# Interleaved chunks that ask for the third quarter last but one, an embedding group in other banks, and the final norm's rows loaded a stage later

## The chip, the core and the metric

The kernel runs on one core of a Trainium2 chip. The metric is device time in microseconds (us) of one execution; lower is better. TensorE (PE) multiplies into PSUM banks; its weight loads are shown apart as PEld. VectorE (DVE) and ScalarE (ACT) do the elementwise work and empty the banks. GpSimd (POOL) and SyncE (SP) here mostly issue DMA transfers.

## The reference, cut to what matters

Two layers over 256 tokens of width 2048, all in fp32. A layer mixes tokens, projects back, adds to the residual, and then adds a per-layer embedding that is gated by a third product of the same width:

```
hn = rmsnorm(h, norm)
u  = hn @ w_in                      # layer 0: 2048 x 6144, layer 1: 2048 x 8208
y  = token mixing of u              # HGRN2 and RG-LRU in layer 0, mLSTM in layer 1
h  = h + y @ w_out                  # 2048 x 2048
pl = rmsnorm(p[i] @ ple_w[i], ple_norm[i])          # 256 -> 2048, the "embedding"
h  = h + sigmoid(h @ ple_gate_w[i]) * pl            # 2048 x 2048, the "gate"
...
return rmsnorm(h, final_norm)
```

## The kernel before, in words

**Products.** A weight arrives as a 128 x 1024 tile `raw` (SP issues the load), is split by ACT into a rounded high part `whi` (L135) and by DVE into the rest `wlo` (L136), and each output is the sum of three products, high by high, high by low and low by high (L196 to L198 in `quarter_tok`, L217 in the seven-product stages). There are four `whi`, four `wlo` and five `raw` buffers. A *chunk* is 512 output columns for the 256 tokens, in two banks (one per 128 tokens); it is built in four *quarters* of the 2048 inputs, 24 matmuls and two weight tiles each.

**Banks.** Of the PSUM banks three form the ring `mm` (pool `pm`), three the ring `mx` (pool `px`), two are `st`. A ring hands out its banks in turn, and a matmul that opens a bank waits until the bank's former contents have been read.

**Stages.** Layer 1 ends with: the gate projections `oog` and `oz` (`seven`, which for each pair of chunks opens banks A, E and B of the `mm` ring and F of the `mx` ring, and whose last results are read out of E and B by L292), the embedding's product (`embed`, L472), the projection back (`out_proj` over the weights `oo`), and the last gate (weights `g1`). `embed` makes four column groups, each with one bank per half of the tokens: eight bank fillings of six matmuls. The first half's bank is copied out by ACT (L483), the second's by DVE (L481).

**Interleaved chunks.** A stage whose inputs come from the stage before cannot have them all at its start: the token-major results are transposed by DVE (L519, L649), sent to DRAM and back by POOL's transfers (`across`, L636 and L639), and turned by ACT and DVE into the split `act` pairs (L667, L149, L150 for `feature_major`; L535, L537 for `to_features`). So `project_two` works on the first two chunks at once, one in `mm` banks and one in `mx` banks, and `before(kq)` (made by `ready`) forces the pairs of quarter kq into the program before the first quarter that reads them. Five stages use it, by way of `chunks`: `eo` and `g0` of layer 0, `oqk`, `oo` and `g1` of layer 1.

**Order.** Small generators called lanes do this side work. `pump` advances each lane one step, once in each quarter, and a lane that has sent its transfers lets `lag` steps go by before it converts what comes back. The framework's scheduler then gives each engine one fixed order of instructions, from the order of the program and from priorities (the weight splits stand 400 places ahead, the embedding's copies 450). An engine works strictly down its list: an instruction that waits holds up all behind it. The lane `fm2` is the third of layer 1's four transposed results (the inputs of quarter 2 of `oo`), `fm3` the fourth. The lane `emb` squares the embedding (L402), multiplies it by its gain rows (L1413, the rows loaded by L503 on POOL's queue) and, before the change, ends by loading the final norm's two rows `fnr` with the same L503.

Of the kernel before, what the change touches and what calls it, by code (L numbers as in the profile page):

```python
# [43 lines left out]
def trunk(ctx: ExitStack, tc: tile.TileContext, a, out):  # L44
# [19 lines left out]
    def start(lane, gen):  # L64
        lanes.setdefault(lane, []).append(gen)
# [16 lines left out]
    def drain(*which):  # L82
        for lane in which:
            while step(lane):
                pass
# [84 lines left out]
    def project_two(w, act, before):  # L170

        ps = [[pool.tile([P, 512], F32, name=name, tag=name) for _ in range(2)]
              for pool, name in ((pm, "mm"), (px, "mx"))]
        for j, kq in ((0, 0), (0, 1), (0, 2), (1, 0), (1, 1), (1, 2), (0, 3), (1, 3)):
            before(kq)
            quarter_tok(w, j, kq, act, ps[j])
            if kq == 3:
                yield ps[j]

    def chunks(w, n, act, before):  # L180
        yield from project_two(w, act, before)
        for j in range(2, n):
            yield project_tok(w, j, act)
# [261 lines left out]
    def embed(w, pact, tile_of, first=None):  # L445

        pls = []
        for b in range(2):
            head = first and b == 0
            if head:  # L450
                part, pact = load_head(w[0])
                parts = [part] + load_weights(w[0], (1, 2), (1,))
            else:
                parts = load_weights(w[b], *(((2, 1),) if first else ()))
            if first and b:
                first()
            for c, (hi, lo) in enumerate(parts):
                terms = [(hf, k, x, y, 0, 512) for hf in range(2) for k in range(2) for x, y in ((0, 0), (0, 1), (1, 0))]
                if head:
                    terms.sort(key=(lambda t: (t[3], t[3] and t[0], t[1])) if c == 0 else  # L460
                               (lambda t: (t[1], t[3] if t[1] == 0 else t[0], t[3])))
                    if c == 0:
                        terms[0:4] = [(hf, 0, x, 0, o, T) for o in (0, T) for x in range(2) for hf in range(2)]
                pool, name = (px, "mx") if first and c == 0 else (pm, "mm")
                ps = [pool.tile([P, 512], F32, name=name, tag=name) for _ in range(2)]
                halves = []
                for n, (hf, k, x, y, o, w_) in enumerate(terms):
                    mine = [m for m, t in enumerate(terms) if t[0] == hf]
                    with ExitStack() as behind:
                        if first and "pe" in last:  # L470
                            behind.enter_context(tc.issue_after(last["pe"]))
                        last["pe"] = te.matmul(ps[hf][:, o:o + w_], tokens(pact[x], k, hf),  # L472
                                               (hi, lo)[y][:, k * 512 + o:k * 512 + o + w_],
                                               start=(n == mine[0]), stop=(n == mine[-1])).ins
                    if n < mine[-1]:
                        continue
                    pl = tile_of()
                    with ExitStack() as order:
                        order.enter_context(tc.high_priority(offset=600 if first else 450))
                        if hf and (b or not first):  # L480
                            ins = v.tensor_copy(pl, ps[hf]).ins  # L481
                        else:
                            ins = s.copy(pl, ps[hf]).ins  # L483
                        if not first:
                            last["out", hf] = ins
                    halves.append(pl)
                pls.append(halves)
        return pls
# [9 lines left out]
    def row(pool, tag, bufs, i):  # L498

        halves = []  # L500
        for b in range(2):
            t = pool.tile([P, 1024], F32, name="row", tag=tag, bufs=bufs)
            gp.dma_start(out=t, in_=a["rows"][i, b * 1024:(b + 1) * 1024].partition_broadcast(P))  # L503
            halves.append(t)
        return halves
# [8 lines left out]
    def to_features(h, c, act, gain, name, more=None):  # L514

        w = room("w")
        w5 = w.rearrange("p (j c h t) -> p h c j t", j=4, c=4, h=2)
        for hf in range(2):
            v.transpose(w5[:, hf], h[:, hf].rearrange("p (c j q) -> p c j q", c=4, j=4))  # L519
        r = room("r")  # L520
        yield from across(w, r, f"d{name}{c}", 6)
        r5 = r.rearrange("p (i c h t) -> p c h i t", i=4, c=4, h=2)
        for b in range(2):
            if gain:
                x = tp.tile([P, 512], F32, name="xr", tag="hn", bufs=3)
                for k in range(2):
                    s.activation(x[:, k * T:(k + 1) * T].rearrange("p (h i t) -> p h i t", h=2, i=4), r5[:, 2 * b + k],
                                 AF.Copy, scale=pc(gain, 4 * c + 2 * b + k))
                act[2 * c + b] = split_act(x, "h")
            else:  # L530
                hi, lo, both = act_pair()
                for k in range(2):
                    src = r5[:, 2 * b + k]
                    hk, lk = (x[:, k].rearrange("p (h i t) -> p h i t", h=2, i=4) for x in (hi, lo))
                    s.copy(hk, src)  # L535
                    for hf in range(2):
                        v.tensor_tensor(out=lk[:, hf], in0=src[:, hf], in1=hk[:, hf].bitcast(F32), op=ALU.subtract)  # L537
                act[2 * c + b] = (hi, lo, both)
        if more is not None:
            yield  # L540
            more(c, r5)

    def ready(act, lane):

        def before(kq):
            while 2 * kq + 1 not in act:
                step(f"{lane}{kq}")
        return before
# [111 lines left out]
    def feature_major(u, gain, first, y, lag):  # L660

        r = yield from landed((u[:, 0], u[:, 1]), f"du{gain}{first}", lag)
        r5 = r.rearrange("p (i c h t) -> p c h i t", i=4, c=4, h=2)
        for b in range(2):
            x = tp.tile([P, 512], F32, name="xr", tag="hn", bufs=3)
            for k in range(2):
                s.activation(x[:, k * T:(k + 1) * T].rearrange("p (h i t) -> p h i t", h=2, i=4), r5[:, 2 * b + k],  # L667
                             AF.Copy, scale=pc(gain, first + 2 * b + k))
            y[first // 2 + b] = split_act(x, "y")
# [55 lines left out]
    if True:  # L725
# [285 lines left out]
        y = {}  # L1011
# [117 lines left out]
    with tc.tile_pool(name="m1", bufs=2) as m1:  # L1129
# [229 lines left out]
        for jj in (0, 2):  # L1359
            us = [m1.tile([P, 2, 512], F32, name="u", tag="vt", bufs=6) for _ in range(2)]  # L1360
            for b, hf, src in pair(a["oz"], jj, not jj):
                j, u = jj + b, us[b]
                with tc.high_priority(offset=100):
                    s.activation(u[:, hf], src, AF.Tanh, scale=norm["rth"][:, hf:hf + 1])
                    v.scalar_tensor_tensor(u[:, hf], u[:, hf], 1.0, src, op0=ALU.add, op1=ALU.mult)
                for i in range(2):
                    c = hf * 8 + 2 * j + i
                    e = slice(i * 256, (i + 1) * 256)
                    v.scalar_tensor_tensor(u[:, hf, e], u[:, hf, e], fac[:, c:c + 1], nums[j][:, hf, e],
                                           op0=ALU.mult, op1=ALU.mult)  # L1370
                if hf:
                    start(f"fm{j}", feature_major(u, "cn", 4 * j, y, 5 + jj // 2))
        hq = []

        def home():
# [23 lines left out]
        def embed_norm():  # L1399
            yield  # L1400
            yield from ple_gain_squares()
            v.tensor_scalar(rp, rsqrt_cols(total(pss, 4)), 0.5, None, op0=ALU.mult)
            fnr.extend(row(m1, "vt", 6, 2))

        def ple_gain_squares():
            rows = row(m1, "vt", 6, 1)
# [18 lines left out]
        def gated(n, ps, tr, pl, hf, on_act=True):  # L1425
# [8 lines left out]
            else:  # L1434
# [2 lines left out]
                sq = tp.tile([P, 512], F32, name="sq", tag="sq", bufs=1)[:, 0:pl.shape[1]]  # L1437
                v.scalar_tensor_tensor(sq, pl, 1.0, pl, op0=ALU.mult, op1=ALU.mult, accum_out=o)

        warm = tp.tile([P, 1], F32, name="warm", tag="warm", bufs=1)  # L1440
        for g, ps in enumerate(chunks(a["g1"], 3, act, ready(act, "fo"))):
            for hf in range(2):
                pl = pls[g][hf]
                gated(g, ps[hf], hq[g][:, hf], pl, hf)
                v.tensor_tensor(out=pl, in0=pl, in1=fnr[g // 2][:, (g % 2) * 512:(g % 2 + 1) * 512], op=ALU.mult)
# [190 lines left out]
```

## Time and profile before

| | |
|---|---|
| time, median of 3 runs | 1029.7 us (1029.24 to 1032.07) |
| the profiled execution: time | 1030.27 us |
| its span, first to last instruction | 1028.5 us |
| PE busy | 1016.8 us (99%) |
| DVE, ACT, POOL busy | 796.4, 623.7, 101.7 us |
| granted TensorE clock, mean | 0.998 |
| DMA | 241.09 MB, mean 234 GB/s |

The profiled execution's time is its span and 1.77 us around it. In a timeline each row gives start, duration, engine, source line, operation, tiles, shape and count; the bracket says how long the engine sat idle before it and what ended that. Consecutive matmuls overlap in their records, so the pace of PE is read from start to start.

### The profile page before, as it was taken

What the parts mean: (1) busy time and instruction counts of PE and PEld (TensorE: products, weight loads), DVE (VectorE), ACT (ScalarE), POOL (GpSimd) and SP (SyncE); (2) the same over time, 40 slices, a digit from 0 to 9 for tenths busy, and PEclk for the clock granted to TensorE, in tenths of its full rate; (3) what the DMA queues carried; (4) which work ended last, traced back from release to release, by engine and by line L of the source; (5) the groups of instructions that cost most, each with busy time, mean ns of one, the idle gap of its engine ahead of it and who ended that gap; (6) DMA issues with size and microseconds to landing.
All of it is one profiled execution on the core that took longest, in us unless ns stands there. A gap on an engine that the chain in (4) does not pass through costs nothing.

```text
span 1028.5 us, 14493 instructions
## 1 busy us (share of the span) xinstructions
PE 1016.8 (99%) x5194; PEld 843.4 (82%) x5194; DVE 796.4 (77%) x1212; ACT 623.7 (61%) x893; POOL 101.7 (10%) x186
## 2 busy tenths in 40 slices
PE   9999999999999999999999999999999999999996
PEld 7888888888888888888888888887888878888886
DVE  7858968969685785767559987888999976766684
ACT  7675555686964345565457776666666666344562
POOL 0111101011112121021021100001011112111000
PEclk9999999999999999999999999999999999999999
DMA  9987756567688897798798756376975779798652
GB/s 360 336 243 231 220 172 204 174 197 236 227 264 291 275 286 230 237 302 256 228 284 244 237 173 203 127 246 173 286 182 170 235 248 348 230 304 255 197 185 82
DMA packets 69384, 241.09 MB, mean 234 GB/s; under 512 B 8992, under 2 KB 10400, under 8 KB 69312
## 3 DMA queue, kind: packets, MB, share of 16 engines
q1 hardware_dynamic: 55008, 194.41, 57.8%
q0 software_dynamic: 13872, 45.23, 15.4%
q8 instruction: 40, 0.66, 0.3%
q10 hardware_dynamic: 432, 0.52, 0.1%
q14 instruction: 32, 0.26, 0.1%
HBM read 220.21 MB, written 19.92 MB: 233 GB/s over the span
## 4 chain that ended last, share of the span: by engine, by line
PE 95%; DMA 2%; issue 1%; ACT 1%; DVE 0%; POOL 0%; ACTq 0%; DVEq 0%; POOLq 0%
PE mm L196 21%; PE mm L197 21%; PE mm L198 21%; PE mm L217 10%; PE mx L198 4%; PE mx L196 4%; PE mx L197 4%; PE mx L217 3%; PE nu L1277 1%; PE mm L1461 1%; PE mm L1462 1%; PE mm L1460 1%; DMA r<-ducn 1%; PE mm L472 1%; DMA ducn<-w 1%
## 5 line engine op out<-in xcount | busy, mean ns | idle before, releaser
L136 DVE TENSOR_TENSOR wlo<-raw,whi 128x1024 fp32r<-128x1024 f32 (+1 forms) x333 | 401.6, 1214 | 156.1 <-ACT whi L135 147.3
L135 ACT CAST whi<-raw 128x1024 fp32r<-128x1024 f32 (+1 forms) x333 | 347.8, 1048 | 262.5 <-PE mm L198 189.6
L196 PE MATMUL mm<-whi,ahl 128*128 128x512 f32 x960 | 375.2, 391 | 0.0
L197 PE MATMUL mm<-wlo,ahl 128*128 128x512 f32 x960 | 374.0, 390 | 0.0
L198 PE MATMUL mm<-whi,ahl 128*128 128x512 f32 x960 | 373.6, 389 | 0.0
L196 PEld LDWEIGHTS mm<-whi,ahl 128*128 128x128 f32 x960 | 180.2, 188 | 38.2 <-issue 0.8
L198 PEld LDWEIGHTS mm<-whi,ahl 128*128 128x128 f32 x960 | 180.2, 188 | 37.6
L197 PEld LDWEIGHTS mm<-wlo,ahl 128*128 128x128 f32 x960 | 180.3, 188 | 37.3 <-DVE wlo L136 0.6
L217 PE MATMUL mm<-whi,ahl 128*128 128x512 f32 x288 | 91.1, 389 | 0.0
L217 PEld LDWEIGHTS mm<-whi,ahl 128*128 128x128 f32 x288 | 54.1, 188 | 11.1
L196 PE MATMUL mx<-whi,ahl 128*128 128x512 f32 x160 | 62.2, 389 | 0.0
L197 PE MATMUL mx<-wlo,ahl 128*128 128x512 f32 x160 | 62.2, 389 | 0.0
L198 PE MATMUL mx<-whi,ahl 128*128 128x512 f32 x160 | 62.2, 389 | 0.0
L217 PE MATMUL mm<-wlo,ahl 128*128 128x512 f32 x144 | 56.2, 390 | 0.4 <-DVE wlo L136 0.4
L207 DVE TENSOR_TENSOR wlo<-ch,whi 128x1024 fp32r<-128x1024 f32 x34 | 41.0, 1220 | 6.0 <-ACT whi L206 5.4
L206 ACT CAST whi<-ch 128x1024 fp32r<-128x1024 f32 x34 | 35.6, 1052 | 6.4 <-PE mm L217 3.7
L198 PEld LDWEIGHTS mx<-whi,ahl 128*128 128x128 f32 x160 | 30.0, 188 | 6.2
L197 PEld LDWEIGHTS mx<-wlo,ahl 128*128 128x128 f32 x160 | 30.0, 188 | 6.2
L196 PEld LDWEIGHTS mx<-whi,ahl 128*128 128x128 f32 x160 | 30.0, 188 | 6.2
L217 PE MATMUL mx<-whi,ahl 128*128 128x512 f32 x104 | 34.4, 390 | 0.0
L217 PEld LDWEIGHTS mm<-wlo,ahl 128*128 128x128 f32 x144 | 27.0, 188 | 6.7 <-DVE wlo L136 1.1
L217 PE MATMUL mm<-whi,q 128*128 128x512 f32 x96 | 32.2, 389 | 0.0
(370 smaller groups left out, 1113.4 us busy)
## 6 DMA issues: line engine op xcount, KB each, us to landing
raw<-in_ew_dram SPq DMA_DIRECT2D x64, 512.0 KB, 5.1
raw<-in_g_dram SPq DMA_DIRECT2D x64, 512.0 KB, 4.6
raw<-in_eo_dram SPq DMA_DIRECT2D x32, 512.0 KB, 5.5
raw<-in_oqk_dram SPq DMA_DIRECT2D x32, 512.0 KB, 5.0
raw<-in_ov_dram SPq DMA_DIRECT2D x32, 512.0 KB, 4.4
raw<-in_oo_dram SPq DMA_DIRECT2D x32, 512.0 KB, 5.8
raw<-in_oog_dram SPq DMA_DIRECT2D x24, 512.0 KB, 4.4
raw<-in_oz_dram SPq DMA_DIRECT2D x24, 512.0 KB, 5.2
```

Source lines behind the costliest of these rows:

```text
L135: last["act"] = s.copy(h, r).ins
L136: last["dve"] = v.tensor_tensor(out=l, in0=r, in1=h.bitcast(F32), op=ALU.subtract).ins
L196: te.matmul(ps[hf], xh, wh, start=(k == 0), stop=False)
L197: te.matmul(ps[hf], xh, wl, start=False, stop=False)
L198: last["pe"] = te.matmul(ps[hf], xl, wh, start=False, stop=(k == KT - 1)).ins
L206: last["act"] = s.copy(hi, r).ins
L207: last["dve"] = v.tensor_tensor(out=lo, in0=r, in1=hi.bitcast(F32), op=ALU.subtract).ins
L217: last["pe"] = te.matmul(o, x, y, start=(first and k + i == 0), stop=(end and k == n - 1 and i == 2), skip_group_check=True).ins
L472: last["pe"] = te.matmul(ps[hf][:, o:o + w_], tokens(pact[x], k, hf), (hi, lo)[y][:, k * 512 + o:k * 512 + o + w_], start=(n == mine[0]), ...
L1277: te.matmul(ps[:, 0:n], x[:, i, o:o + P], y[:, b, i], start=(b == 0 and x is sh and y is vh), stop=(b == hf and y is vl))
L1460: te.matmul(o, xh, wh, start=(k == 0), stop=False)
L1461: te.matmul(o, xh, wl, start=False, stop=False)
```

## The change

It has five parts:

1. `project_two` takes the first two chunks' quarters in the order 0, 1 of the first, 0, 1 of the second, then 2 of both and 3 of both. Before, quarter 2 of the first chunk came third; now it comes fifth.
2. The second layer's embedding puts its first column group into `mx` banks, as the first layer's already does; the other three groups stay in `mm` banks.
3. `to_features` subtracts for both halves of the tokens in one DVE instruction in place of two.
4. `feature_major` for the last two results of layer 1 (`fm2`, `fm3`) waits 5 steps of the pump in place of 6.
5. The final norm's rows are loaded by a lane of their own that starts with the last gate's stage, and no longer by the lane `emb`.

```diff
-        for j, kq in ((0, 0), (0, 1), (0, 2), (1, 0), (1, 1), (1, 2), (0, 3), (1, 3)):
+        for j, kq in ((0, 0), (0, 1), (1, 0), (1, 1), (0, 2), (1, 2), (0, 3), (1, 3)):
             before(kq)
             quarter_tok(w, j, kq, act, ps[j])
...
-                pool, name = (px, "mx") if first and c == 0 else (pm, "mm")
+                pool, name = (px, "mx") if c == 0 and (first or b == 0) else (pm, "mm")
...
-                    for hf in range(2):
-                        v.tensor_tensor(out=lk[:, hf], in0=src[:, hf], in1=hk[:, hf].bitcast(F32), op=ALU.subtract)
+                    v.tensor_tensor(out=lk, in0=src, in1=hk.bitcast(F32), op=ALU.subtract)
...
-                    start(f"fm{j}", feature_major(u, "cn", 4 * j, y, 5 + jj // 2))
+                    start(f"fm{j}", feature_major(u, "cn", 4 * j, y, 5))
...
             v.tensor_scalar(rp, rsqrt_cols(total(pss, 4)), 0.5, None, op0=ALU.mult)
-            fnr.extend(row(m1, "vt", 6, 2))
...
+        def final_rows():
+            yield
+            fnr.extend(row(m1, "vt", 6, 2))
+
+        start("fnr", final_rows())
         warm = tp.tile([P, 1], F32, name="warm", tag="warm", bufs=1)
         for g, ps in enumerate(chunks(a["g1"], 3, act, ready(act, "fo"))):
+            drain("fnr")
```

The instruction lists change in few places. On ACT, between the `oz` stage and the `oo` stage, where `pl` is the embedding, `u` the gated value of `oz`, and `xr` the conversion of `fm2`'s transposed values, before:

```order
L483 COPY pl<-mm 128x512
L1364 ACTIVATE u<-pr,rth 128x512
L135 CAST whi<-raw 128x1024
L483 COPY pl<-mm 128x512
L667 ACTIVATE xr<-r,prm 128x256 x3
L135 CAST whi<-raw 128x1024
L149 CAST ahl<-xr 128x2x256
L483 COPY pl<-mm 128x512
L667 ACTIVATE xr<-r,prm 128x256
```

and with the change (the lines below the edits have numbers one lower, L1363 for L1364):

```order
L483 COPY pl<-mx 128x512
L1363 ACTIVATE u<-pr,rth 128x512
L135 CAST whi<-raw 128x1024
L483 COPY pl<-mm 128x512
L135 CAST whi<-raw 128x1024
L483 COPY pl<-mm 128x512
L135 CAST whi<-raw 128x1024
L483 COPY pl<-mm 128x512
L135 CAST whi<-raw 128x1024
L402 ACTIVATE sq,pss<-pl 128x512 x2
L135 CAST whi<-raw 128x1024 x2
L666 ACTIVATE xr<-r,prm 128x256 x3
```

The conversion of `fm2` moved from behind the second copy of the embedding to behind the fourth, with five weight splits and two squares more ahead of it.

On DVE in the same place, where `pr` is bank B of `oz` being read out, `pl` the embedding and `u` the gated value with its factor, before:

```order
L292 TENSOR_TENSOR pr<-mm,pr 128x512
L136 TENSOR_TENSOR wlo<-raw,whi 128x1024
L481 COPY pl<-mm 128x512
L1365 SCALAR_TENSOR_TENSOR u<-u,pr 128x512
L136 TENSOR_TENSOR wlo<-raw,whi 128x1024
L1369 SCALAR_TENSOR_TENSOR u<-u,fac,num 128x256
L481 COPY pl<-mm 128x512
L1369 SCALAR_TENSOR_TENSOR u<-u,fac,num 128x256 x2
L136 TENSOR_TENSOR wlo<-raw,whi 128x1024
L649 STREAM_TRANSPOSE w<-u 128x4x4x32
L481 COPY pl<-mm 128x512
```

and with the change:

```order
L292 TENSOR_TENSOR pr<-mm,pr 128x512
L136 TENSOR_TENSOR wlo<-raw,whi 128x1024
L481 COPY pl<-mx 128x512
L1364 SCALAR_TENSOR_TENSOR u<-u,pr 128x512
L136 TENSOR_TENSOR wlo<-raw,whi 128x1024
L1368 SCALAR_TENSOR_TENSOR u<-u,fac,num 128x256
L481 COPY pl<-mm 128x512
L1368 SCALAR_TENSOR_TENSOR u<-u,fac,num 128x256
L136 TENSOR_TENSOR wlo<-raw,whi 128x1024
L1368 SCALAR_TENSOR_TENSOR u<-u,fac,num 128x256
L648 STREAM_TRANSPOSE w<-u 128x4x4x32
L481 COPY pl<-mm 128x512
```

Nothing moved here but one of the last two factor instructions, which now stands behind a weight split; the first copy reads an `mx` bank.

On POOL at the end of the program, where `dfo` and `r` are the transposed results of `oo` on their way through DRAM, before:

```order
L639 DMA r<-dfo_8122 32x4x256 x4
L503 DMA row<-in_rows_dram 128x1024 x2
L636 DMA dfo_8194<-w 128x1024
L639 DMA r<-dfo_8194 32x4x256 x4
L636 DMA dfo_8352<-w 128x1024
```

and with the change, at the very end of the list:

```order
L635 DMA dfo_8332<-w 128x1024
L638 DMA r<-dfo_8332 32x4x256 x4
L635 DMA dfo_8510<-w 128x1024
L638 DMA r<-dfo_8510 32x4x256 x4
L503 DMA row<-in_rows_dram 128x1024 x2
```

The two row loads moved from behind the first to behind the fourth of these results.

## The prediction

> **What bounds the kernel now.** I read the page's totals and clock row first:
>
> ```profile
> span 1028.5 us, 14493 instructions
> PE 1016.8 (99%) x5194; PEld 843.4 (82%) x5194; DVE 796.4 (77%) x1212; ACT 623.7 (61%) x893; POOL 101.7 (10%) x186
> PEclk9999999999999999999999999999999999999999
> ```
>
> PE is busy throughout at the full granted clock. The change leaves its matmuls as many and as large, so it can win only time in which PE stands still. The list of PE's waits is next:
>
> ```profile
> PE mm L472 <- ACT pl L483: 1.0, 1, 1.0
> PE st L97 <- PEq L1627: 0.8, 1, 0.8
> PE mm L472 <- DVE pr L292: 0.5, 1, 0.5
> PE mm L217 <- DVE wlo L136: 0.4, 1, 0.4
> PE mx L472 <- ACT whi L441: 0.4, 1, 0.4
> ```
>
> That is all of it. The interleaved stages (L196 to L198) are not in it: none of the five waits for its quarters. Two of the five entries, L472 at 1.0 and 0.5, are the second layer's embedding. The rest is the start of the program and one weight split in `oz`, which the change leaves alone. The timeline of PE shows the embedding's real loss, from start to start, since the records overlap:
>
> ```profile
> 832.00 0.39 PE L472 MATMUL mm<-whi,ahl 128*128 128x512 f32 x1
> ...
> 834.50 0.39 PE L472 MATMUL mm<-whi,ahl 128*128 128x512 f32 x1
> 835.43 0.47 PE L472 MATMUL mm<-whi,ahl 128*128 128x512 f32 x1 [0.54 <-DVE pr L292]
> 835.73 0.40 PE L472 MATMUL mm<-wlo,ahl 128*128 128x512 f32 x1
> 835.96 0.62 PE L472 MATMUL mm<-whi,ahl 128*128 128x512 f32 x2
> ...
> 842.09 0.39 PE L472 MATMUL mm<-whi,ahl 128*128 128x512 f32 x1
> 843.48 0.50 PE L472 MATMUL mm<-whi,ahl 128*128 128x512 f32 x1 [1.00 <-ACT pl L483]
> ...
> 844.98 0.46 PE L196 MATMUL mm<-whi,ahl 128*128 128x512 f32 x1
> ```
>
> The pace without a wait is read off the chain of work that ended last, whose pieces are start, length and count:
>
> ```profile
> 680.28 5.44 PE mm L217 x24
> ...
> 688.44 1.36 PE mm L217 x6
> ```
>
> One bank takes 6 matmuls, 1.36 us; a quarter takes 24, 5.44 us. The embedding's eight banks should take 8 x 1.36 = 10.88 us, and they take 844.98 - 832.00 = 12.98. So 2.10 us are lost, in two places: the third bank opens late at 835.43 and the eighth at 843.48. That is the largest gain the bank and lag edits can have here.
>
> **The two stalls, and why.** ACT's timeline, then DVE's:
>
> ```profile
> 835.94 1.04 ACT L135 CAST whi<-raw 128x1024 fp32r<-128x1024 f32 x1
> 837.07 0.59 ACT L483 COPY pl<-mm 128x512 f32<-128x512 f32 x1
> 840.18 1.31 ACT L667 ACTIVATE xr<-r,prm 128x256 f32<-128x256 f32 x3 [2.52 <-DMA r<-ducn]
> ...
> 842.34 0.61 ACT L149 CAST ahl<-xr 128x512 fp32r<-128x512 f32 x1
> 842.85 0.58 ACT L483 COPY pl<-mm 128x512 f32<-128x512 f32 x1
> ```
>
> ```profile
> 834.59 0.69 DVE L292 TENSOR_TENSOR pr<-mm,pr 128x512 f32<-128x512 f32 x1
> 835.20 1.22 DVE L136 TENSOR_TENSOR wlo<-raw,whi 128x1024 fp32r<-128x1024 f32 x1
> 836.33 0.69 DVE L481 COPY pl<-mm 128x512 f32<-128x512 f32 x1
> 836.93 0.68 DVE L1365 SCALAR_TENSOR_TENSOR u<-u,pr 128x512 f32<-128x512 f32 x1
> 837.53 1.22 DVE L136 TENSOR_TENSOR wlo<-raw,whi 128x1024 fp32r<-128x1024 f32 x1
> 838.66 0.48 DVE L1369 SCALAR_TENSOR_TENSOR u<-u,fac,num 128x256 f32<-128x256 f32 x1
> 839.06 0.68 DVE L481 COPY pl<-mm 128x512 f32<-128x512 f32 x1
> ...
> 843.60 0.70 DVE L649 STREAM_TRANSPOSE w<-u 128x512 f32<-128x512 f32 x1
> ```
>
> First stall: the embedding begins on the `mm` ring A, E, B just after `oz` has filled E and B. Its third bank is B, and DVE reads B only from 834.59 to 835.28. Second stall: the eighth bank reuses the fifth's, which PE had filled by 839.5 (835.43 and three banks). Its copy stood on ACT behind the conversion `xr`, which waited for `fm2`'s transfer until 840.18, and started at 842.85.
>
> **Bank edit.** The first two fillings go to `mx` banks. The last reader of one there, by its line's first and last start, is 15 us earlier:
>
> ```profile
> L292 DVE TENSOR_TENSOR pr<-mx,pr x4: 682/683/685, 692.4 to 817.2; 128x512 f32<-128x512 f32 x4
> ```
>
> So they open at 832.00 without a wait. Then follow A at 834.72, E at 836.08, B at 837.44, A at 838.80, E at 840.16, B at 841.52, and the stage `oo` at 842.88. I check each opening with the steps of the rows above. B is read by 835.28: 2.2 us early. The second A needs ACT's copy of the first, which stands where the copy at 837.07 did: 837.66, in time. The second E needs DVE's second copy, 839.06 to 839.74: 0.4 early. The last opening is the tight one: `oo` reuses A, filled by 840.16 and copied by DVE's third L481. From 839.66, with starts spaced as above (factor 0.40, split 1.13, factor 0.40, transpose some 0.65), that copy runs from 842.24 to 842.92. From the end of L292 at 835.28 PE took 0.15 to start, and its next step was 0.30 in place of 0.23. So I estimate 0.2 lost there: 0.04 + 0.15.
>
> **Lag and order edits, at `oo`.** Parts 1 and 4 together put `xr` behind the fourth copy. ACT then has only weight splits between the last copies, and they wait for PE to free a `whi`, at PE's own pace: the third copy can end 0.59 after its bank is full at 838.80, near 839.4, for a bank wanted at 841.52, the fourth likewise near 842.1 for one wanted at 842.88 + 2.72 = 845.6. `xr` comes after the sixth split of the `oo` weights:
>
> ```profile
> 850.71 1.06 ACT L135 CAST whi<-raw 128x1024 fp32r<-128x1024 f32 x1 [0.30 <-PE mm L198]
> ```
>
> It would start at 849.9 (851.77 less the gain), long after the transfer, and end some 4 us later (three `xr` 1.31, casts 0.61 each, a fourth `xr` and a square between). Quarter 2 is now read fifth, at 842.88 + 4 x 5.44 = 864.6. So about 11 us of cover, where quarter 2 read third (853.8) would have had next to none. That is what part 1 is worth here: it covers the later conversion. In the other four stages no wait is listed, and their ACT lists are unchanged: zero.
>
> **One subtraction in place of two, and the final rows.**
>
> ```profile
> L537 DVE TENSOR_TENSOR ahl<-r,ahl 128x128 fp32r<-128x128 f32 x64 | 13.9, 281 | 1.8 <-ACT ahl L535 1.8
> ```
>
> Sixty-four instructions become 32. The new shape has no row; it costs between one old one (281 ns) and the pair (562), so DVE saves between 0 and 9.0 us in all. DVE is not waited for in these stages, which hides both ends: zero. The final rows are issued behind the last `dfo` transfer, and are first read by L1445 in the middle of the last gate:
>
> ```profile
> 942.09 2.18 POOL L639 DMA_DIRECT2D r<-dfo  x4 [5.62 <-DMA dfo<-w]
> ...
> L1445 DVE TENSOR_TENSOR pl<-pl,row x6: 683/686/694, 971.3 to 1002.5; 128x512 f32<-128x512 f32 x6
> ...
> DMA to landing us min/median/max: 5.8/8.2/10.7
> ```
>
> Issued by 945.4 and landed after at most 10.7 us, they are there at 956, 15 us before use. Queued last on POOL, they delay nothing behind them: zero.
>
> **Sum.** 2.10 - 0.2 = 1.9 us off. Nothing after `oo` opens waits before or after, so the gain stays: span 1026.6, execution 1030.27 - 1.9 = 1028.4. The profiled execution lies 0.57 above the median of the runs shown; from that median, 1029.7 - 1.9 = **1027.8**. The ends of the copy terms: nothing lost (gain 2.1), or a copy as late as the second stall's (gain about 0.9).
>
> **Rivals.** *A copy is late somewhere else.* If DVE's third copy or ACT's third slips by 1 us, one stall of the old size, 2.10 less 0.9, stays: 1028.8. Against it: the margins above are 2 us and more on ACT; on DVE the second copy has 0.4 and the third none.
>
> *The embedding's gain rows become the wait: slower.*
>
> ```profile
> 862.39 1.29 DVE L1413 TENSOR_TENSOR pl<-pl,row 128x512 f32<-128x512 f32 x2 [3.93 <-DMA row<-in_rows_dram]
> 863.61 2.36 DVE L136 TENSOR_TENSOR wlo<-raw,whi 128x1024 fp32r<-128x1024 f32 x2
> ...
> 867.05 0.39 PE L197 MATMUL mx<-wlo,ahl 128*128 128x512 f32 x1
> ```
>
> DVE stands 3.93 us before L1413, with the splits of `oo`'s fifth quarter queued behind it. From landing to the first split's end is 1.22 + 1.23 us, and PE wants that split at 867.05, or 865.15 with the gain. So a landing up to 862.7 costs nothing, each microsecond beyond costs one. Before it was 862.39; since the row loads stand on POOL behind `fm3`'s transposed result, whose first transpose moves from 843.60 to some 841.6, I expect 860.5. The gain is gone at 864.6. Past 867.7 the kernel is slower by over 3.1 us, say 1033.5 with a landing at 868.2. That asks for 7 us more than expected, and landings spread over 4.9 (5.8 to 10.7).
>
> *The change does not do what it says:* the stalls' cause is a transfer and a split that stand as late as before, and the banks only move the wait: 1029.7. Against it, both named releasers are bank reads.
>
> *Each pause costs more than itself.* Had PE run at half pace for one bank after each of the two openings, 2 x 1.36 us more would be there to win: 1025.1. Against it: from 835.73 on the steps are 0.23 again, and the 29 steps from 835.43 to 842.09 average 0.230. The Trainium skill's page "TensorE: Matmul & The Clock Gate", section "A second HAM failure mode: psum-queue depth-cycling", says that short idles between bank groups can throttle the clock again and again, and that the throughput pays for each warming up. With its window of about 3.4 us at half clock my estimate by that page would be 1.7 us per pause, 1024.4; the clock row and these steps do not bear it out.
>
> **How the numbers follow.** Forecast 0.73; late copy 0.11; rows 0.08 (half of it slower); no effect 0.05; costly pauses 0.03. Within 0.3% (3.1 us, about what a measurement of this kernel can tell from no change) lie the forecast, the late copy, the no effect and half the rows. The runs shown spread over 2.8 us, so 0.04 of the forecast falls to faster, 0.01 to slower: faster 0.07, same 0.88, slower 0.05. Range: below, the lowest run shown (1029.24) less the full 2.10, and once more the 0.57 by which one execution here lay off the median, 1026.5; above, no gain and the same 0.57, 1030.3, which takes in a late landing that costs up to 2.5.
>
> **What would show it.** Right: L472 in PE's waits at or under 0.3; first L196 of `oo` near 843.0; no `xr` wait on ACT between the embedding's copies; L1413's wait still ended ahead of PE's need; span 1026.6. Wrong: an entry of 0.5 or more for L472 or L196 behind `pl`, any L197 behind `wlo` around 865, or a pace under 0.227 per step after the pauses.

## The result, and the profile after

| | before | after |
|---|---|---|
| median of 18 runs each, in turn on the same chip | 1030.93 us | 1028.74 us |
| lowest to highest | 1028.68 to 1032.36 | 1027.97 to 1030.96 |
| ratio, 95% interval | | 0.9983 [0.9976, 0.9991] |
| span of the profiled execution | 1028.5 us | 1026.3 us |
| first matmul of the embedding (L472) to first of `oo` (L196) | 12.98 us | 10.88 us |
| first matmul of `oo` to the last matmul of the program | 174.69 us | 174.60 us |

By the ratio the change is worth 0.17% of 1030.9 us, 1.8 us (0.9 to 2.5); by the two spans 2.2 us. The forecast was 1.9 us off, 1027.8 us from the lower median known then, with a range of 1026.5 to 1030.3.

The page's totals and clock row of the changed kernel:

```profile
span 1026.3 us, 14463 instructions
PE 1016.2 (99%) x5194; PEld 843.8 (82%) x5194; DVE 794.4 (77%) x1180; ACT 623.1 (61%) x893; POOL 101.7 (10%) x186
PEclk9999999999999999999999999999999999999998
```

The matmuls are as many as before, PE has no work less, only fewer waits, and DVE has 32 instructions and 2.0 us of busy time less. The list of PE's waits has no entry of the second layer's embedding any more. The L472 that is left is at the start of the program, and so is the L197 (16.39 us):

```profile
PE st L97 <- PEq L1631: 0.8, 1, 0.8
PE mx L472 <- ACT whi L441: 0.3, 1, 0.3
PE mm L217 <- DVE wlo L136: 0.3, 1, 0.3
PE mm L197 <- DVE wlo L136: 0.2, 1, 0.2
```

PE's timeline, first and third bank of the embedding and first matmul of `oo` (start, length, instruction):

```profile
832.00 0.39 PE L472 MATMUL mx<-whi,ahl 128*128 128x512 f32 x1
...
834.72 0.39 PE L472 MATMUL mm<-whi,ahl 128*128 128x512 f32 x1
...
842.65 0.39 PE L472 MATMUL mm<-whi,ahl 128*128 128x512 f32 x1
842.88 0.39 PE L196 MATMUL mm<-whi,ahl 128*128 128x512 f32 x1
```

The embedding starts at the same 832.00 as before. That is chance: the other profiled executions below start it between 831.06 and 836.25, so their stages are compared by lengths and not by instants. Its third bank opens at 834.72 in place of 835.43, and `oo` at 842.88 in place of 844.98: 8 x 1.36 us, no step lost. ACT in the same place, with the third and fourth copy and then the conversion of `fm2`:

```profile
839.00 0.59 ACT L483 COPY pl<-mm 128x512 f32<-128x512 f32 x1 [0.26 <-PE mm L472]
840.40 1.05 ACT L135 CAST whi<-raw 128x1024 fp32r<-128x1024 f32 x1 [0.82 <-PE mm L472]
841.72 0.59 ACT L483 COPY pl<-mm 128x512 f32<-128x512 f32 x1 [0.26 <-PE mm L472]
...
849.48 1.30 ACT L666 ACTIVATE xr<-r,prm 128x256 f32<-128x256 f32 x3
```

The copies wait for PE and nothing else. `xr` starts with no wait in brackets, 6.6 us after `oo` has opened. DVE has the late reader of bank B, the copy on which `oo`'s opening rests, and the gain rows:

```profile
834.21 0.68 DVE L292 TENSOR_TENSOR pr<-mm,pr 128x512 f32<-128x512 f32 x1
...
841.83 0.65 DVE L481 COPY pl<-mm 128x512 f32<-128x512 f32 x1
...
861.59 1.29 DVE L1411 TENSOR_TENSOR pl<-pl,row 128x512 f32<-128x512 f32 x2 [5.00 <-DMA row<-in_rows_dram]
```

The copy ends at 842.48, 0.40 ahead of `oo`. The rows land at 861.59, and no L197 waits behind the splits that follow. The single subtraction (its group: busy us, mean ns, idle before) and the last gate's rows on POOL and where they are first used:

```profile
L536 DVE TENSOR_TENSOR ahl<-r,ahl 128x256 fp32r<-128x256 f32 x32 | 11.4, 411 | 0.0
```

```profile
942.24 1.11 POOL L503 DMA_DIRECT2D row<-in_rows_dram  x2
```

```profile
L1449 DVE TENSOR_TENSOR pl<-pl,row x6: 684/685/693, 969.1 to 1001.5; 128x512 f32<-128x512 f32 x6
```

The L217 in the list is the weight split of before, at 714.94 now. The prediction puts it into `oz`; it stands in `oog`, since the first weights of `oz` are loaded at 729 us. One new subtraction takes 411 ns against 281 for each of the old pair, and the rows are issued some 26 us before they are used.

### The profile page after: what moved, and what is told of

It is laid out like the page before. It is cut to its first block, busy times and chain, and to the rows that moved or that the text cites. A ratio compares the mean times of both kernels' runs of the same rounds, so it can differ in the third digit from the quotient of the medians.

```text
span 1026.3 us, 14463 instructions
## 1 busy us (share of the span) xinstructions
PE 1016.2 (99%) x5194; PEld 843.8 (82%) x5194; DVE 794.4 (77%) x1180; ACT 623.1 (61%) x893; POOL 101.7 (10%) x186
## 4 chain that ended last, share of the span: by engine, by line
PE 97%; ACT 1%; DMA 1%; DVE 1%; issue 0%; ACTq 0%; DVEq 0%
PE mm L196 21%; PE mm L197 21%; PE mm L198 21%; PE mm L217 12%; PE mx L198 4%; PE mx L196 4%; PE mx L197 4%; PE mx L217 3%; PE nu L1276 1%; PE mm L472 1%; DMA raw<-in_pw_dram 1%; PE mm L1466 1%; PE mm L1464 1%; PE mm L1465 1%; PE mx L785 0%; DVE wlo L136 0%
## 5 line engine op out<-in xcount | busy, mean ns | idle before, releaser
L196 PE MATMUL mm<-whi,ahl 128*128 128x512 f32 x960 | 375.1, 391 | 0.0
L197 PE MATMUL mm<-wlo,ahl 128*128 128x512 f32 x960 | 374.0, 390 | 0.2 <-DVE wlo L136 0.2
L196 PEld LDWEIGHTS mm<-whi,ahl 128*128 128x128 f32 x960 | 180.2, 188 | 38.1 <-issue 0.8
L197 PEld LDWEIGHTS mm<-wlo,ahl 128*128 128x128 f32 x960 | 180.2, 188 | 37.6 <-DVE wlo L136 0.9
L217 PE MATMUL mm<-whi,ahl 128*128 128x512 f32 x288 | 91.1, 389 | 0.0
L217 PEld LDWEIGHTS mm<-whi,ahl 128*128 128x128 f32 x288 | 54.1, 188 | 11.2
L196 PE MATMUL mx<-whi,ahl 128*128 128x512 f32 x160 | 62.2, 389 | 0.0
L197 PE MATMUL mx<-wlo,ahl 128*128 128x512 f32 x160 | 62.2, 389 | 0.0
L217 PE MATMUL mm<-wlo,ahl 128*128 128x512 f32 x144 | 56.3, 391 | 0.3 <-DVE wlo L136 0.3
L207 DVE TENSOR_TENSOR wlo<-ch,whi 128x1024 fp32r<-128x1024 f32 x34 | 41.0, 1220 | 6.0 <-ACT whi L206 5.4
L197 PEld LDWEIGHTS mx<-wlo,ahl 128*128 128x128 f32 x160 | 30.1, 188 | 6.3
L196 PEld LDWEIGHTS mx<-whi,ahl 128*128 128x128 f32 x160 | 30.1, 188 | 6.2
L217 PE MATMUL mx<-whi,ahl 128*128 128x512 f32 x104 | 34.4, 390 | 0.0
L217 PEld LDWEIGHTS mm<-wlo,ahl 128*128 128x128 f32 x144 | 27.0, 188 | 6.5 <-DVE wlo L136 1.0
L217 PE MATMUL mm<-whi,q 128*128 128x512 f32 x96 | 32.1, 389 | 0.0
```

The costliest lines, as they stand in the source:

```text
L196: te.matmul(ps[hf], xh, wh, start=(k == 0), stop=False)
L197: te.matmul(ps[hf], xh, wl, start=False, stop=False)
L207: last["dve"] = v.tensor_tensor(out=lo, in0=r, in1=hi.bitcast(F32), op=ALU.subtract).ins
L217: last["pe"] = te.matmul(o, x, y, start=(first and k + i == 0), stop=(end and k == n - 1 and i == 2), skip_group_check=True).ins
```

## Experiments

The parts have the numbers of the list in "The change". Ratios are to the kernel before, timed in turn on the same chip, whose median moved between 1029.8 and 1030.9 from call to call. Ratios are therefore compared, not medians.

| run | what it has | median us | ratio, 95% interval | embedding us | `oo` to last matmul us |
|---|---|---|---|---|---|
| changed kernel | 1 to 5 | 1028.74 | 0.9983 [0.9976, 0.9991] | 10.88 | 174.60 |
| e1 | 2 | 1030.07 | 1.0000 [0.9989, 1.0011] | 10.88 | 174.61 |
| e2 | 1 | 1030.05 | 0.9992 [0.9981, 1.0003] | 12.41 | 174.60 |
| e3 | 1, 2 | 1029.25 | 0.9987 [0.9977, 0.9998] | 11.35 | 176.44 |
| e4 | 3, 4, 5 | 1029.85 | 0.9996 [0.9985, 1.0007] | 12.54 | 174.71 |
| e5 | all, gain rows late | 1035.03 | 1.0045 [1.0030, 1.0060] | 11.18 | 180.97 |
| e6 | 2, `fm2` late | 1034.87 | 1.0044 [1.0028, 1.0059] | 11.57 | 181.09 |
| e7 | all, `fm2` late | 1028.81 | 0.9990 [0.9980, 1.0001] | 10.88 | 174.61 |
| e8 | all, gain rows early | 1028.67 | 0.9985 [0.9976, 0.9994] | 10.88 | 174.61 |
| e9 | e8, gates of `oog` later | 1028.31 | 0.9985 [0.9974, 0.9996] | 11.14 | 174.74 |
| e10 | all but 1 | 1029.88 | 0.9998 [0.9989, 1.0007] | 11.92 | 174.72 |
| e11 | all but 2 | 1028.87 | 0.9986 [0.9977, 0.9994] | 11.29 | 174.61 |

The last two columns are from one profiled execution each, the ratios from 4 to 18 runs. The profiled execution need not be a typical one: those of e1 and e4 were the fastest of their kernel's runs, that of e9 the slowest.

### e1: the banks alone

The kernel before with the one line of part 2.

> Only part 2 (the first group in mx banks). Theory A, the place of xr decides: the first opening no longer waits, but on ACT the third copy still stands behind xr and its transfer (landed near 840.1), so it starts near 842.85 and the eighth opening waits for it as before, near 843.5. L196 of oo starts near 845.0 as before, one stall of about 2.0 us in place of 0.70 and 1.16; span 1028.4, time as before within 0.3 us. Theory B, each stall is the price of its own bank: the first 0.70 us is won, L196 near 844.3, span 1027.8.

Measured: ratio 1.0000, no gain in the median; yet the profiled execution, span 1026.4 us, shows no stall in the embedding. ACT's timeline tells why, with the old order of its list:

```profile
838.04 1.31 ACT L667 ACTIVATE xr<-r,prm 128x256 f32<-128x256 f32 x3 [0.66 <-DMA r<-ducn]
839.26 1.04 ACT L135 CAST whi<-raw 128x1024 fp32r<-128x1024 f32 x1
840.20 0.61 ACT L149 CAST ahl<-xr 128x512 fp32r<-128x512 f32 x1
840.71 0.58 ACT L483 COPY pl<-mm 128x512 f32<-128x512 f32 x1
```

`xr` still stands ahead of the third copy, but `fm2`'s transfer landed at 838.04, 5.97 us after the embedding's first matmul (832.07), where the kernel before had 8.18. From the landing to the copy's end are 3.25 us, so the copy ended at 841.29, and the eighth bank, wanted near 841.6, opened in time. The expected stall did not come in this execution: the profile caught an early landing, in the fastest of the twelve runs, and the timed runs as a whole gained nothing. Where `fm2`'s transfer landed in the other eleven was not recorded.

### e2 and e3: the order alone, and the order with the banks

e2 is the kernel before with the one line of part 1, e3 has the lines of parts 1 and 2.

> Only part 1 (the order of the quarters). Theory A: xr leaves its place ahead of the third copy, the eighth opening does not wait, the first stall of 0.70 us (third bank open at 835.43, behind L292 of bank B) stays; L196 of oo near 843.6 to 843.7, span 1027.1, 1.4 us faster than before. Theory B, the lag (part 4) is what moves xr: L196 near 845.0, span 1028.4, no gain.

> Parts 1 and 2 without 3, 4 and 5. Theory A: the whole gain, no L472 in PE's waits, L196 of oo at 842.9, span 1026.3, ratio 0.998 to before. Theory B, part 4 or the shorter DVE lists have a share: 0.3 us or more is missing, span 1026.6 or over.

Measured for e2: ratio 0.9992, no stall at the eighth bank, and the one at the third left, which is larger than before's. PE, then ACT 10 us earlier:

```profile
836.60 0.47 PE L472 MATMUL mm<-whi,ahl 128*128 128x512 f32 x1 [1.26 <-DVE pr L292]
```

```profile
825.95 1.31 ACT L667 ACTIVATE xr<-r,prm 128x256 f32<-128x256 f32 x3 [3.07 <-DMA r<-ducn]
```

That earlier `xr` is `fm1`'s conversion. DVE's split of its result, two weight splits and both readings of `oz`'s banks stand behind it in a row, so the reading of bank B (L292) starts 9.8 us after `xr` in all thirteen profiled executions. The first stall, too, follows a transfer's landing; the prediction had put it down to DVE's list alone. No run moved `fm1`'s transfer on purpose.

Measured for e3: ratio 0.9987. Its profiled execution shows the rival that the prediction called the gain rows (DVE, then PE):

```profile
864.67 1.29 DVE L1413 TENSOR_TENSOR pl<-pl,row 128x512 f32<-128x512 f32 x2 [5.89 <-DMA row<-in_rows_dram]
865.89 0.68 DVE L150 TENSOR_TENSOR ahl<-xr,ahl 128x512 fp32r<-128x512 f32 x1
866.49 2.35 DVE L136 TENSOR_TENSOR wlo<-raw,whi 128x1024 fp32r<-128x1024 f32 x2
```

```profile
867.76 0.50 PE L197 MATMUL mm<-wlo,ahl 128*128 128x512 f32 x1 [1.40 <-DVE wlo L136]
```

The rows landed at 864.67, and PE waited 1.40 us for the split behind them. In e3, which lacks parts 3 to 5, `fm2`'s conversion stands a quarter later on ACT (856.25, 12.2 us after `oo` opened, against 6.6), and the L150 that belongs to it falls between the gains and the split: 0.60 of the wait. In the embedding 0.47 us were lost too (11.35), at the two banks for which the prediction had the least margin: 0.22 at the seventh, behind DVE's second copy, which ran until 840.90, and 0.25 at `oo`, which opened at 844.08 behind the third copy's end at 844.02.

### e4: the other three parts

Parts 3, 4 and 5 as in the diff of the change, without 1 and 2.

> Parts 3, 4 and 5 without 1 and 2. Theory A: nothing; L196 of oo near 845.0, span 1028.4, ratio 1.000 within 0.0007, although DVE has 32 instructions fewer and the final rows move. Theory B, DVE's shorter lists or the rows' later transfer give some of the gain: span 1028.0 or less.

Measured: ratio 0.9996, and both stalls are there. The first opening waited 1.04 us for L292, the eighth bank opened 0.20 late behind `xr`, which landed at 838.79. The three parts by themselves gain nothing that can be measured.

### e5: the gain rows late

In the changed kernel the first gain row is loaded twice, so the rows land later.

```diff
             rows = row(m1, "vt", 6, 1)
+            gp.dma_start(out=rows[0], in_=a["rows"][1, 0:1024].partition_broadcast(P))
```

> The changed kernel, with the first of the embedding's two gain rows loaded a second time behind the first transfer, so that it is there some 8 us later (near 870). DVE's list then has L1412 in front of the splits of oo's sixth quarter, which PE wants at 870.3. Theory A, the rows can become PE's wait: DVE stands before L1412 until the landing, four gains, two casts and a split follow (4.9 us), PE waits in L197 for wlo until landing + 4.9, some 4 us; time 1032 to 1034, 2 to 5 us slower than before's gain allows. Theory B, rows are hidden whenever they land: no wait of L197, span 1026.3, time near 1028.7.

Measured: 1035.03 us, ratio 1.0045. The kernel is slower than before, and by more than the 1032 to 1034 expected. DVE, then PE:

```profile
869.43 1.29 DVE L1412 TENSOR_TENSOR pl<-pl,row 128x512 f32<-128x512 f32 x2 [7.08 <-DMA row<-in_rows_dram]
```

```profile
870.72 0.39 PE L196 MATMUL mx<-whi,ahl 128*128 128x512 f32 x1
874.33 0.79 PE L197 MATMUL mx<-wlo,ahl 128*128 128x512 f32 x1 [3.22 <-DVE wlo L136]
874.92 0.63 PE L198 MATMUL mx<-whi,ahl 128*128 128x512 f32 x1
875.34 0.63 PE L196 MATMUL mx<-whi,ahl 128*128 128x512 f32 x1
...
879.61 0.63 PE L197 MATMUL mx<-wlo,ahl 128*128 128x512 f32 x1
880.04 0.47 PE L198 MATMUL mx<-whi,ahl 128*128 128x512 f32 x1
880.35 0.40 PE L196 MATMUL mx<-whi,ahl 128*128 128x512 f32 x1
```

PE stood 3.61 us from start to start in place of 0.23, and then made 12 steps of 0.427 us, nearly twice the usual 0.227, until 880.04. From 874.33 to 880.35 are 14 steps in 6.02 us, 2.84 more than at full pace. Wait and slow steps make 3.38 + 2.84 = 6.2 of the 6.4 us by which `oo` to the last matmul grew.

### e6 and e7: `fm2`'s transfer late, with the old order and with the new

The write of `fm2` to DRAM is made twice, ahead of the reads: in e6 with the banks alone, in e7 in the changed kernel.

```diff
+        if name == "ducn8":
+            gp.dma_start(out=d, in_=w)
```

> Part 2 alone, with fm2's transposed values written to DRAM twice, so that they land some 6 us later, near 844.3. xr stands on ACT ahead of the embedding's fourth copy. Theory A, a conversion ahead of a copy costs when its transfer is late: the copy ends near 846.7, and PE, which wants its bank at 845.6 for the second half of oo's first quarter, waits about 1 us; the wait is longer by each microsecond that the landing is later. L196 or the embedding shows up in PE's waits. Theory B, with the first group in mx banks no copy is ever late: no such wait, span 1026.4.

> The changed kernel with the same doubled write of fm2's values. xr now stands behind all four copies and behind the sixth oo split, near 849.5. Theory A, part 1's order covers the transfer: no wait of ACT on the transfer or under 1 us, no PE wait in the embedding, L196 at 842.9; time within 1 us of the changed kernel, unless the doubled write on POOL's queue makes the gain rows late too (L1412 then waits, and L197 behind it). Theory B, the late transfer costs as much as in the kernel with part 2 alone.

Measured for e6: 1034.87 us, ratio 1.0044. ACT and PE:

```profile
848.13 0.51 ACT L669 ACTIVATE xr<-r,prm 128x256 f32<-128x256 f32 x1 [9.08 <-DMA r<-ducn]
...
849.89 0.56 ACT L483 COPY pl<-mm 128x512 f32<-128x512 f32 x1
```

```profile
845.66 0.39 PE L198 MATMUL mm<-whi,ahl 128*128 128x512 f32 x1
850.50 0.70 PE L196 MATMUL mm<-whi,ahl 128*128 128x512 f32 x1 [4.45 <-ACT pl L483]
851.00 0.63 PE L197 MATMUL mm<-wlo,ahl 128*128 128x512 f32 x1
...
853.99 0.42 PE L198 MATMUL mm<-whi,ahl 128*128 128x512 f32 x1
```

In this kernel the conversion came to stand behind the third copy and ahead of the fourth, so the wait fell on `oo`'s second bank: 4.84 us from start to start, then seven steps of 0.427 us. About 1 us had been expected, of a landing near 844.3; it came at 848.13. Measured for e7: 1028.81 us, ratio 0.9990, no wait of PE outside the program's start and `oog`, embedding 10.88. ACT's `xr` started without a wait behind the copies:

```profile
849.08 1.30 ACT L668 ACTIVATE xr<-r,prm 128x256 f32<-128x256 f32 x3
```

With the doubled write e6 lost 6.5 us of `oo` in its profiled execution, and 0.44% by the ratio where e1, with the same parts, lost nothing. e7, the changed kernel with it, lost nothing in its profiled execution and nothing that can be told from the noise by the ratio. Two more things differ between the kernels than part 1: e7 has parts 3 to 5 as well, and its transposed reads were issued 5.3 us after the embedding's first matmul (836.86), those of e6 7.5 us after it (838.97). e7's landed 5.6 to 7.6 us after their issue, the last by some 846, later than before's 840.18 and ahead of `xr` at 849.08. So this pair shows plainly that the place behind the copies covers a later transfer, and not what a delay like e6's would cost there.

### e8: the gain rows early

```diff
+        gain_rows = row(m1, "vt", 6, 1)
...
-            rows = row(m1, "vt", 6, 1)
+            rows = gain_rows
```

The first line stands ahead of the embedding, so the rows are issued on POOL ahead of `fm3`'s transfer.

> The changed kernel, with the embedding's gain rows loaded before the embedding, ahead of fm3's transposed result on POOL's queue. Theory A, in the median execution the rows are close to PE's need or past it (0.8 us of slack in the changed kernel's profile, 1.4 us late in the profile with parts 1 and 2): DVE no longer waits before L1412, no L197 waits near 865, span 1026.3 or a little less, and the median is 0.3 to 1.0 us below the changed kernel's 1028.7. Theory B, the rows' wait is always hidden: nothing but the 5 us of DVE idle goes, median 1028.7.

Measured: DVE reaches the gains at 857.12 and waits for nothing:

```profile
857.12 1.29 DVE L1412 TENSOR_TENSOR pl<-pl,row 128x512 f32<-128x512 f32 x2
```

Ratio 0.9985 against the changed kernel's 0.9983: no gain in the median, so a late landing of the rows is not what most executions of the changed kernel pay for. The eleven runs lie between 1027.64 and 1029.25, where the changed kernel's eighteen reached 1030.96. That this is the rows' doing was not shown.

### e9: a version meant to beat both

e8, and the gates made of `oog`'s results one instruction later on DVE (the `mixed_gates()` call moved ahead of the next entry, a second one added behind the stage, and both issued behind DVE's last weight split), so that they no longer stand ahead of the split that PE waits for at 714 us.

> The changed kernel, with the embedding's gain rows loaded before the embedding, as in the run with early rows, and with the gates of the output projection issued one instruction later on DVE, so that its numerators no longer stand ahead of the weight split that PE waits for at 714 us. Theory A (the only stalls left are that split, 0.56 us here, and the rows' chance of a late landing): PE's wait for wlo at L217 is gone from the list, the profiled span is 0.3 to 0.6 below the changed kernel's, near 1025.8, the median of the runs near 1028.2 to 1028.5. Theory B (DVE's work that is moved back comes due at the next split or the next bank's opening): another wait of 0.4 to 0.6 at L217 or L198 stands in its place, and the time is that of the changed kernel, 1028.7.

Measured: median 1028.31 us, ratio 0.9985, and with this interval no better than the changed kernel. The profiled execution was the slowest of the twelve (1032.72, span 1030.9). It shows another transfer that landed late, the embedding's inputs, on ACT and then PE:

```profile
712.03 0.62 ACT L149 CAST ahl<-praw 128x512 fp32r<-128x512 f32 x1 [4.78 <-DMA praw<-in_pT_dram]
```

```profile
713.65 0.50 PE L217 MATMUL mm<-whi,q 128*128 128x512 f32 x1 [2.30 <-ACT whi L206]
714.91 0.51 PE L217 MATMUL mm<-wlo,q 128*128 128x512 f32 x1 [0.76 <-DVE wlo L207]
```

The edit has a share in it. SP issues this transfer once DVE is done with L241, which in e9's list comes behind a moved gate and a split (L1344, L207): SP waited 4.1 us for it, 1.9 in e8. The rest is the transfer itself, which landed 8.1 us after its issue in place of e8's 3.1. So the profile says nothing on the wait that was to go (0.56 us with the slow step behind it), and whether the edit removes it stays open.

### e10 and e11: all but the order, all but the banks

Each is the changed kernel with the one line of part 1, or of part 2, as it was before.

> The changed kernel with the old order of the interleaved chunks (third quarter read third), so parts 2, 3, 4 and 5 without part 1. Theory A (part 1 covers the conversion of fm2, whose transfer lands at another time in each execution): ACT has the conversion between the embedding's second and third copy again, and the embedding's eighth bank opens late by as much as the landing is later than about 838.3 us, 0 to 1.9; embedding 10.9 to 12.8 us; the median of the runs 0.5 to 1.3 above the changed kernel's, near 1029.6. Theory B (the order is worth nothing once the first fillings go to other banks): no wait on ACT's third copy in any case, embedding 10.9, the median that of the changed kernel, 1028.7.

> The changed kernel with the embedding's first two fillings in the mm banks again, so parts 1, 3, 4 and 5 without part 2. Theory A (each of the two edits takes away one stall, and they add up): the third bank opens late again behind DVE's reading of bank B, by 0.7 to 1.6 us, the eighth opens in time; embedding 11.6 to 12.5 us; the median of the runs 0.7 to 1.5 above the changed kernel's, near 1029.8. Theory B (the order alone carries the whole gain, since the run without it lost 1.1 us): the late opening is made good at a later bank, where PE would have waited anyway; embedding 10.9 to 11.2, the median 1028.7.

Measured for e10: ratio 0.9998, so without the order no gain is left that can be told from none. ACT has the conversion between the copies again, and PE waits for the third copy:

```profile
841.01 1.31 ACT L666 ACTIVATE xr<-r,prm 128x256 f32<-128x256 f32 x3 [1.68 <-DMA r<-ducn]
...
843.68 0.57 ACT L483 COPY pl<-mm 128x512 f32<-128x512 f32 x1
```

```profile
844.31 0.50 PE L472 MATMUL mm<-whi,ahl 128*128 128x512 f32 x1 [0.74 <-ACT pl L483]
```

From `xr`'s start to the copy's end are again 3.24 us. Measured for e11: ratio 0.9986, where 0.9990 or more had been expected of two stalls that add up. In this execution L292 came early, and the third bank's opening was only 0.29 us late (835.10 for 834.82, inside a merged row of PE's timeline; the embedding took 11.29). DVE's rows:

```profile
834.27 0.69 DVE L292 TENSOR_TENSOR pr<-mm,pr 128x512 f32<-128x512 f32 x1
...
836.00 0.69 DVE L481 COPY pl<-mm 128x512 f32<-128x512 f32 x1
```

What the banks add to the order is too small for these medians, and lies by the profiled executions between 0.4 us (e11) and 1.5 us (e2).

**The two stalls, put together.** The table counts from the embedding's first matmul; a loss is a step less 0.23. "-" is a conversion behind the copies.

| kernel | banks, order | `xr` of `fm1` | L292 on bank B | third bank late | `xr` of `fm2` | eighth bank late |
|---|---|---|---|---|---|---|
| before | old, old | -7.23 | 2.59 | 0.70 | 8.18 | 1.16 |
| e4 | old, old | -6.73 | 3.09 | 1.20 | 7.73 | 0.20 |
| e2 | old, new | -6.51 | 3.32 | 1.42 | - | 0 |
| e11 | old, new | -7.65 | 2.18 | 0.29 | - | 0 |
| e1 | new, old | -7.37 | 2.45 | 0 | 5.97 | 0 |
| e10 | new, old | -7.25 | 2.58 | 0 | 7.13 | 0.90 |
| changed | new, new | -7.62 | 2.21 | 0 | - | 0 |

Four rows with the old banks: the loss at the third bank is L292's start less 1.89, to 0.01 us. Three rows with the old order that lost: the eighth bank is opened 3.30 us after `xr`'s start, and it is wanted 9.53 after the first matmul, plus what the third bank was late already with its slow second step (0.08). So the loss there is `xr` - 6.23 less the first loss: for e10 7.13 - 6.23 = 0.90, for before 8.18 - 6.23 - 0.78 = 1.17, for e4 7.73 - 6.23 - 1.28 = 0.22. The two stalls do not add up; the later of two transfers sets the end of the embedding. By this rule, taking away the first alone would have saved nothing in before's execution, since the eighth bank would have waited so much longer; taking away the second alone would have left 0.78.

With the new banks one limit set by `fm1` is left. Where L292 is late, DVE's copies behind it are late too, and `oo` opens 8.32 us after L292's start: in e3, e5, e6 and e9, with L292 at 2.82 to 3.26 us after the first matmul, 8.32 or 8.33 in each. By 10.88 - 8.32 a start up to 2.56 costs nothing. The changed kernel's 2.21 was early enough; e5's and e9's, with all five parts, were not, and lost 0.30 and 0.26.

## Why the prediction was right, point by point

- **Where the loss was, and its size: right.** 2.10 us of PE's standing still in the embedding, all of it gone in the profiled execution, and the ratio's 1.8 us (0.9 to 2.5) hold the 1.9. That the 1.9 lies so near the 1.8 is in part luck. It rests on one execution of before, which lost 2.10; e4, with the same banks and order, lost 1.66 (12.54), and of the six executions with both parts three lost 0.26 to 0.47 (e3, e5, e9). The opening of `oo` at 842.88 was said to be near 843.0, the span 1026.6 where 1026.3 came.
- **The bank edit.** The openings came at the instants worked out. The term of 0.2 us at `oo` was not lost in this execution: DVE's third copy ended at 842.48, since L292 came at 834.21 where the working took before's 834.59. With L292 0.6 to 0.8 later, as in e9, e5 and e3 (2.82, 2.85 and 3.02 after the first matmul, against 2.21), the same place cost 0.24 to 0.25. The term was a price of some executions, not of each.
- **The lag and order edits.** "Parts 1 and 4 together put `xr` behind the fourth copy" was wrong in its division: e2 and e3 have the conversion behind all copies with part 1 and without part 4, and e10 shows that without part 1 part 4 leaves it between the second and the third. Part 4's work is elsewhere: it brings the conversion a quarter (5.4 us) earlier again, which keeps DVE's L150 out of the chain behind the gain rows (`xr` 6.6 to 6.7 us after `oo` opens in the five other kernels with all parts or all but 2, against 12.0 and 12.2 in e2 and e3, which lack parts 3 and 5 too). Of the "about 11 us of cover" e7's later transfer used some, at no cost; how far it reaches was not shown.
- **The sum had a hidden step.** The prediction added two stalls. The table above shows that they are two limits side by side, so neither edit has a price of its own. For both edits together the sum is the same, and so the number stood; for each alone it would have failed, as e11's expectation of two stalls that add up did. e1's expectation had the eighth bank wait the longer once the third did not; its ratio bears that out, its profiled execution, with the early landing, does not show it.
- **The subtraction and the final rows at zero: right.** DVE is busy 11.4 us with the 32 instructions where it was 13.9 with the 64, so 2.5 us less, inside the 0 to 9.0; no wait of PE went with it, and e4's ratio has no gain that can be told from none.
- **The rival of the gain rows: real, and not the usual case.** The landing came at 861.59, 0.8 earlier than before's and not the expected 1.9 (860.5); e3's at 864.67 cost 1.4 us with part 4 left out, e5 shows the full price. The prediction's "each microsecond beyond costs one" left out what follows a long wait: e5 lost 3.38 by the wait and 2.84 by the slow steps behind it.
- **The rival of the costly pauses: against it for the pauses at hand, as e5 and e6 bear out by contrast.** After pauses of 0.9 to 1.7 us in the embedding (before, e2, e4, e10) and 1.8 in e3 the steps were 0.23 at once but for the first one or two; after pauses of 3.6 and 4.8 us they were 0.427. The Trainium skill's page "TensorE: Matmul & The Clock Gate", section "What's actually happening", states half the clock after an idle window of about 3.4 us; the pauses of up to 1.8 us and those of 3.6 and 4.8 agree. The Trainium skill's section on short idles that the prediction weighed, "A second HAM failure mode: psum-queue depth-cycling", speaks of frequent ones; no single pause of up to 1.8 us here bears it out.
- **That the change does nothing, and the late copy:** refuted, the first by the ratio, whose interval ends below 1, the second in the profiled execution, where no copy was late. In e3, e5 and e9 DVE's third copy was late, but by 0.25 us and not by the rival's 1.

## What to carry to other kernels

Where PE waits twice in one stage, work out each limit from the stage's start and take the later one; waits in a row are seldom terms of a sum, and an edit that removes the earlier one alone may only lengthen the other. Look behind the named releaser for the transfer that sets its time: here both stalls moved by a microsecond and more from execution to execution with a landing, so an order that keeps a transfer's reader behind the work PE needs is worth more than a place that fits one trace. One profiled execution gives the mechanism, but what it is worth is told by ratios over many runs: e1's trace showed a full gain that its runs did not have.

## What the hardware showed that was not expected

The price of a PE pause jumps somewhere between 1.8 and 3.6 us. Up to 1.8 us it cost itself and about 0.1 us more; at 3.6 us (e5) 12 steps at 0.427 us followed, at 4.8 us (e6) seven. In e9 two pauses of 2.7 and 1.3 us with a single matmul between them were followed by the same 0.427 us steps (from 715.72 to 718.71); whether the first alone would have done it was not shown. The granted clock of these runs, as a mean over the span, fell only from 0.997 or 0.998 to 0.994 (e5) and 0.996 (e6 and e9), too little to be seen in the clock row's tenths. Taken over the slow steps alone it is 0.50 in e5 (874.3 to 880.0) and e9 (715.7 to 718.7) and 0.52 in e6 (850.5 to 854.0), where it is 1.00 in the 2.6 us behind each of before's two stalls.

The landings spread more than the edits were worth. `fm2`'s transfer landed 5.97 to 8.18 us after the embedding's first matmul in four executions with the old order, `fm1`'s 6.51 to 7.65 us ahead of it in the executions of the table. Issue and transfer both moved: before issued `fm2`'s reads 0.7 us ahead of the first matmul, and they took 7.0 us (median), e4 0.9 us behind it, and they took 3.8. Why they move was not settled. In the five executions with parts 1, 3, 4 and 5 whose early part was left alone (changed, e5, e7, e8, e11) L292 came 1.61 to 2.85 after the first matmul, in those that lack at least one of the four 2.45 to 3.32; with one profiled execution for each kernel that is no proof of an effect.
